# A two-layer hybrid attention trunk on one core: small softmax operations moved to ScalarE

## The chip, the cores and the metric

The kernel runs on 1 core of one Trainium2 chip. The metric is device time in microseconds (us) of one execution; the profile is of one execution, with the time of every instruction on the five engines: TensorE (PE, with its weight loads as PEld), VectorE (DVE), ScalarE (ACT), GpSimd (POOL) and SyncE (SP, which here issues the DMAs).

## What is computed

Two layers of a decoder trunk on 512 tokens of 1024 channels, in float32. Each layer normalizes and modulates its input, projects it once (8608 columns), and feeds two attention branches and their gates:

```python
# branch A: 3 groups of 8 heads x 64, (window, dilation) = (128,1), (512,4), (2048,16)
s = where(valid, q @ k.T * 64**-0.5 + bias, -1e30)
m = max(s); p = exp(s - m); l = sum(p)
o = (p / l) @ v;  lse = m + log(l)
y_a = sum(o * softmax(lse over the 3 groups)) * silu(a_z)
# branch B: 16 heads, 64 + 32 rotary, low-rank q and kv
y_m = softmax(causal((q_nope @ k_nope.T + q_rope @ k_rope.T) * 96**-0.5)) @ v * silu(m_z)
# merge
x = x + gate * ((sigmoid(g_a) * (y_a @ W_a) + sigmoid(g_m) * (y_m @ W_b)) @ W_o)
```

## The kernel before

Every float32 factor of a matmul is kept as two parts, a rounded high part and the difference to it, and a product is three matmuls (line 166). A weight tile of 128 columns is loaded by SP (`stage`, two buffers), its high part `wh` is made on ScalarE or VectorE (lines 203, 205), its low part `wl` mostly on GpSimd by a subtraction of 128x1024 (line 206), and its 24 matmuls of 512 columns go into one of two PSUM banks called `pj`.

The bank is then read out in two parts. For a key of groups 1 and 2 (lines 663 to 667) that is four operations: the high half of head 0 on ScalarE (`kb`, line 211), its low half on VectorE (line 667), then the high half of head 1 (line 213) and its low half (line 667), both on VectorE. Only then can the next but one projection have the bank.

Branch A runs per layer in four pairs of heads, j = 0 to 3 (`a_attn`). `a_scores` makes the scores in `s` banks; VectorE adds the bias, writes `p` and takes the row maxima (lines 782, 800), a small operation scales them by -1/8 into `m0` and `m12` (lines 784, 802), and ScalarE takes the exponential with these as bias (lines 786, 806). `a_factors` joins the three groups. Groups 1 and 2 hold their tokens in another order (by phase p instead of by block qb), so their statistics `ml` (maxima and sums) are reordered by `swap_blocks` into `mn`, and later the factors `fn` into `fp`: 16 copies of 32 partitions each time, 32x4 or 32x2 elements (line 815), dealt to the engines by the string `SW = "GVVV"`: 4 on GpSimd, 12 on VectorE. Between the two swaps stands a chain of small operations of 128x8 elements (lines 834 to 845: `M`, `en`, its exponential on ScalarE at line 838, `L`, `fn`). After the second one `f12` is made and the `p` tiles are scaled (lines 860, 862), transposed (line 869) and multiplied with v.

Branch B runs 16 heads per layer (`m_head`), each in four blocks of rows. Per block VectorE adds the mask and takes the maximum `m` (line 1101), a 128x1 product with the row's scale gives `nms` (line 1102), and ScalarE takes the exponential with it as bias (line 1103).

The order of instructions on each engine is not the order of the code: a list scheduler with a model of the engines sets it when the program is built, and priorities and tile pools steer it. Each engine then works through its own list in order and stops at the first instruction whose inputs are not there.

Of the kernel before, what the change touches and what calls it, by code (L numbers as in the profile page):

```python
# [13 lines left out]
AF = mybir.ActivationFunctionType  # L14
ALU = mybir.AluOpType
# [33 lines left out]
GP = (0, 0, 1, 0, 0)  # L49
KD = "GG"  # L50
LE = "GV"
SW = "GVVV"
YZ = "GGV"
ENG = dict(first="AGAG", qk="AAAG", v="AGAV", az="GGVA", lat="VVGG", mz="VGVA", gate="VAVA", uq="AGGG", ukv="VVAG",
           q="AGAG", y="VGAV", out="AAVV", mr="GGAA", wo="VGVV", K="AAVV", kr="GGGV", sq="AGGG", kv="VA", pk="AV",
# [5 lines left out]
SA = 0.125  # L61
# [76 lines left out]
def trunk(ctx, tc, x, positions, w_ada, w_in, w_uq, w_ukv, w_out_a, w_out_b, w_o, rel_bias, vecs, cst, ohb, bmask, out):  # L138
    nc = tc.nc
    V, A, G, T = nc.vector, nc.scalar, nc.gpsimd, nc.tensor  # L140
# [15 lines left out]
    def t2(tag, dt=F32, shape=(128, 512)):  # L156
        return sb.tile(list(shape), dt, tag=tag, name=nm(tag), bufs=BUFS[tag])

    def small(shape, tag, bufs=2, dt=F32):
        return sb.tile(list(shape), dt, tag=tag, name=nm(tag), bufs=bufs)  # L160

    def bank(tag, dt=F32):
        return ps.tile([128, 512], dt, tag=tag, name=nm(tag), bufs=PB[tag])

    def mm(o, l, r, start, stop):
        T.matmul(o, l, r, start=start, stop=stop, skip_group_check=True)  # L166
# [292 lines left out]
    for t in range(NT):  # L459
        for i in range(2):  # L460
# [12 lines left out]
            for k in range(2):  # L473
                e = V.tensor_copy if k % 2 else A.copy
# [127 lines left out]
    def layer(l, xT, hT):  # L602
# [156 lines left out]
        def a_scores(j, qk, stat):  # L759

            bts = [t2("bias") for _ in range(2)]
            for e in range(2):
                dma(bts[e], btile[2 * j + e])
            m0, l0, m12, l12 = stat
            pps = [[], []]

            def scores(o, q, k):
                mm(o, q[0], k[0], True, False)
                mm(o, q[0], k[1], False, False)
                mm(o, q[1], k[0], False, True)  # L770

            for e in range(2):
                x0 = small([128, 4], "x0")
                sp = [bank("s"), bank("s")]
                pp = [t2("p"), t2("p")]
                for qb, pc, c0, n in G0_BLOCKS:
                    o = sp[pc][:, c0:c0 + n]
                    k0 = 128 * (qb - 1) if n == 256 else 0
                    qt = qk[0][0][e][:, 128 * qb:128 * qb + 128]
                    mm(o, qt, qk[0][1][e][:, k0:k0 + n], True, False)  # L780
                    mm(o, qt, qk[0][1][2][e][:, k0:k0 + n], False, True)
                    V.tensor_tensor_reduce(pp[pc][:, c0:c0 + n], o, bts[e][:, 256 - n:256], 1.0, -3e38,
                                           ALU.add, ALU.max, x0[:, qb:qb + 1])
                V.tensor_scalar(m0[:, e, :], x0, -SA, None, ALU.mult)
                for qb, pc, c0, n in G0_BLOCKS:
                    A.activation(pp[pc][:, c0:c0 + n], pp[pc][:, c0:c0 + n], AF.Exp, bias=m0[:, e, qb:qb + 1],
                                 scale=SA, accum_out=l0[:, e, qb:qb + 1])
                pps[e] += pp
            for g in (1, 2):
                x12 = small([128, 2, 4], "x12")  # L790
                pt = [t2("p"), t2("p")]
                for p2 in range(2):
                    o = bank("s")
                    for p in (2 * p2, 2 * p2 + 1):
                        sl = slice(128 * p, 128 * p + 128)
                        scores(o[:, 256 * (p % 2):256 * (p % 2) + 256], [a[:, sl] for a in qk[g][0]],
                               [a[:, p].rearrange("d e i -> d (e i)") for a in qk[g][1]])
                        for e in range(2):
                            c0 = 256 * (p % 2) + 128 * e
                            V.tensor_tensor_reduce(pt[e][:, sl], o[:, c0:c0 + 128], bts[e][:, 128 + 128 * g:256 + 128 * g],  # L800
                                                   1.0, -3e38, ALU.add, ALU.max, x12[:, e, p:p + 1])
                V.tensor_scalar(m12[:, g - 1], x12, -SA, None, ALU.mult)
                for e in range(2):
                    for p in range(4):
                        sl = slice(128 * p, 128 * p + 128)
                        A.activation(pt[e][:, sl], pt[e][:, sl], AF.Exp, bias=m12[:, g - 1, e, p:p + 1],  # L806
                                     scale=SA, accum_out=l12[:, g - 1, e, p:p + 1])
                    pps[e].append(pt[e])
            return pps

        def swap_blocks(dst, src):
            for qb in range(4):
                for p in range(4):
                    c = SW[(4 * qb + p) % len(SW)]
                    (A.copy if c == "A" else (G if c == "G" else V).tensor_copy)(  # L815
# [39 lines left out]
        def scaled(p, blocks, engines):  # L855

            for (c0, n, f), e in zip(blocks, engines):
                sl = p[:, c0:c0 + n]
                if e == "A":
                    A.activation(sl, sl, AF.Copy, scale=f)  # L860
                else:
                    (V if e == "V" else G).tensor_scalar(sl, sl, f, None, ALU.mult)

        def transposed(srcs):

            n = 128 * len(srcs)
            tp = bank("t")
            for b, s in enumerate(srcs):
                T.transpose(tp[:, 128 * b:128 * b + 128], s, eye)  # L869
            h, lo = t2("pth", F32R), t2("ptl", F32R)  # L870
            hi_copy(h[:, :n], tp[:, :n], "pt")
            V.tensor_tensor(lo[:, :n], tp[:, :n], f32(h[:, :n]), ALU.subtract)  # L872
            return h, lo

        def cols(a, c0):
            return a[:, c0:c0 + 128]

        def pv_block(o, vtile, hh, ph, pl, last):

            c = 128 * hh + 64 * (hh % 2)  # L880
            vh, vl = vtile[:, c:c + 64], vtile[:, c + 64 - 128 * (hh % 2):][:, :64]
            mm(o, vh, ph, False, False)
            mm(o, vh, pl, False, False)
            mm(o, vl, ph, False, last)
# [54 lines left out]
        q_scale = None  # L939
# [145 lines left out]
        def m_head(q, vts, hh):  # L1085
            qh, ql = q
            kh, kl = K[hh]
            m = small([128, 4], "mm")
            ls = small([128, 4], "ml_")
            nms = small([128, 4], "mn_")  # L1090
            sp = [bank("s") for _ in range(3)]
            pp = [t2("p") for _ in range(3)]
            for qb, pc, c0 in M_BLOCKS:
                n = 128 * qb + 128
                o = sp[pc][:, c0:c0 + n]
                qs = slice(128 * qb, 128 * qb + 128)
                mm(o, qh[:, qs], kh[:, :n], True, False)
                mm(o, qh[:, qs], kl[:, :n], False, False)
                mm(o, ql[:, qs], kh[:, :n], False, True)
                pt = pp[pc][:, c0:c0 + n]  # L1100
                V.tensor_tensor_reduce(pt, o, mask[:, 512 - n:512], 1.0, -3e38, ALU.add, ALU.max, m[:, qb:qb + 1])  # L1101
                V.tensor_tensor(nms[:, qb:qb + 1], m[:, qb:qb + 1], q_scale[1][:, qb:qb + 1], ALU.mult)
                A.activation(pt, pt, AF.Exp, bias=nms[:, qb:qb + 1], scale=q_scale[0][:, qb:qb + 1], accum_out=ls[:, qb:qb + 1])
            V.reciprocal(ls, ls)
            for i in range(3):
                scaled(pp[i], [(c0, 128 * qb + 128, ls[:, qb:qb + 1]) for qb, pc, c0 in M_BLOCKS if pc == i], SM[i])
            at = {qb: (pp[pc], c0) for qb, pc, c0 in M_BLOCKS}
            o = bank("o")
            vs = slice(128 * hh, 128 * hh + 128)
            def blocks(kb):  # L1110
                return [cols(at[qb][0], at[qb][1] + 128 * kb) for qb in range(kb, 4)]

            def pv(kb, ph_, pl_, last=False):
                mm(o[:, 128 * kb:], vts[kb][:, vs], ph_, kb == 0, False)
                mm(o[:, 128 * kb:], vts[kb][:, vs], pl_, False, last)

            h, lo = transposed(blocks(0))
            pv(0, h, lo)
            h, lo = transposed(blocks(1) + blocks(3))
            pv(1, h[:, :384], lo[:, :384])  # L1120
            pv_block(o[:64, 384:], vts[3], hh, h[:, 384:], lo[:, 384:], False)
            h, lo = transposed(blocks(2))
            pv(2, h[:, :256], lo[:, :256], True)
            return o
# [90 lines left out]
        for n in range(16):  # L1215
            q, i, e = n // 4, n // 2 % 2, n % 2
# [31 lines left out]
        for c2 in range(4):  # L1248
            parts = []
            for a, wv, yv, tag in ((0, w_out_a, yar, "zs"), (1, w_out_b, ymr, "yy")):  # L1250
                gs = []
                for i in range(2):
                    col = 256 * c2 + 128 * i
                    g = t2(tag)
# [119 lines left out]
```

## Time and profile before

| | us |
|---|---|
| median of 3 runs | 1466.23 |
| lowest, highest | 1463.68, 1473.56 |
| the profiled execution: its own time | 1475.04 |
| the profiled execution: span of its instructions | 1473.3 |

Times below come from the profiled execution, in us from the start of its span. Busy shares of its span: PE 92%, DVE 69%, ACT 42%, POOL 41%. [...] Branch A lies at about 140 to 450 us in layer 0 and 850 to 1150 in layer 1, the heads of branch B at 450 to 625 and 1150 to 1325.

### The profile page before, as it was taken

To read this page: it belongs to the slowest core of one execution; us is meant where nothing else is said; L and a number is where in the kernel's file an instruction comes from. 1 tells how busy PE (TensorE), PEld (TensorE's weight loads), DVE (VectorE), ACT (ScalarE), POOL (GpSimd) and SP (SyncE) were. 2 spreads that over 40 slices of the span, in tenths; PEclk is the share of its full clock that TensorE was granted. 3 is DMA by queue.
4 is the path that set the end of the run, shared out by engine and by line. 5 is a ranking of instruction groups with operands and counts; after the bars stand their busy time and mean duration, and the time that the engine had idled before them with its cause. 6 is when DMAs were issued, how large, how long until landed. Compare 5 with 4: busy or idle time off the path is not lost.

```text
span 1473.3 us, 21395 instructions
## 1 busy us (share of the span) xinstructions
PE 1355.9 (92%) x7327; PEld 1164.8 (79%) x7327; DVE 1011.8 (69%) x2477; ACT 624.0 (42%) x1493; POOL 602.9 (41%) x495
## 2 busy tenths in 40 slices
PE   4998798999998999999988999899999899999997
PEld 4787686897887777888888987689788777787877
DVE  7788769346766788855689347734676688885563
ACT  3424552335345767621034254333534576762101
POOL 5423435334563342345434344523456334234530
PEclk7999999999999999999999999999999999999998
DMA  9676414323244333455644232223324433345541
GB/s 323 224 241 187 142 44 122 90 79 86 58 129 116 96 84 111 128 173 164 202 150 131 81 97 73 79 77 90 88 58 129 118 95 86 99 127 186 166 138 58
DMA packets 236677, 181.48 MB, mean 123 GB/s; under 512 B 16410, under 2 KB 204224, under 8 KB 236568
## 3 DMA queue, kind: packets, MB, share of 16 engines
q1 hardware_dynamic: 236568, 180.11, 40.8%
q8 instruction: 58, 0.95, 0.3%
q14 instruction: 51, 0.42, 0.1%
HBM read 150.60 MB, written 23.17 MB: 118 GB/s over the span
## 4 chain that ended last, share of the span: by engine, by line
PE 59%; DVE 22%; DMA 6%; ACT 5%; issue 4%; POOL 3%; SPq 1%; DVEq 0%; ACTq 0%; POOLq 0%
PE pj L166 41%; PE s L166 12%; PE o L166 4%; PE t L869 3%; ACT p L806 2%; DVE mn L815 2%; DMA stage<-in_w_o 2%; POOL wl L206 2%; DVE p L1101 1%; DVE lat L286 1%; DVE ptl L872 1%; DMA v<-in_w_ada 1%; DVE wh L205 1%; DVE fp L815 1%; DVE kb L1043 1%
## 5 line engine op out<-in xcount | busy, mean ns | idle before, releaser
L206 POOL TENSOR_TENSOR wl<-stage,wh 128x1024 fp32r<-128x1024 f32 (+1 forms) x134 | 316.3, 2361 | 350.7 <-ACT wh L203 184.7
L166 PE MATMUL pj<-hTh,wh 128*128 128x512 f32 (+1 forms) x864 | 346.2, 401 | 49.3 <-DVE kb L667 24.8
L166 PE MATMUL pj<-hTl,wh 128*128 128x512 f32 (+1 forms) x864 | 340.4, 395 | 0.0
L166 PE MATMUL pj<-hTh,wl 128*128 128x512 f32 (+1 forms) x848 | 336.7, 397 | 0.0
L166 PEld LDWEIGHTS pj<-hTh,wh 128*128 128x128 f32 x864 | 166.9, 193 | 87.7 <-issue 36.9
L166 PEld LDWEIGHTS pj<-hTl,wh 128*128 128x128 f32 x864 | 166.9, 193 | 32.7 <-issue 0.3
L166 PEld LDWEIGHTS pj<-hTh,wl 128*128 128x128 f32 x848 | 164.2, 194 | 29.1 <-issue 0.2
L203 ACT ACTIVATE wh<-stage 128x1024 fp32r<-128x1024 f32 (+1 forms) x84 | 85.1, 1014 | 151.2 <-PE s L166 62.5
L872 DVE TENSOR_TENSOR ptl<-t,pth 128x512 fp32r<-128x512 f32 (+2 forms) x160 | 95.9, 615 | 42.1 <-ACT pth L211 41.6
L211 ACT ACTIVATE pth<-t 128x512 fp32r<-128x512 f32 (+2 forms) x160 | 80.8, 537 | 60.1 <-PE t L869 58.9
L166 PE MATMUL s<-kb,qh 128*128 128x256 f32 (+3 forms) x384 | 86.2, 317 | 9.3 <-DVE mm L1101 3.6
L166 PE MATMUL o<-pth,v 128*64 128x128 f32 (+3 forms) x496 | 88.6, 255 | 2.9 <-DVE kh L923 1.9
L166 PE MATMUL o<-ptl,v 128*64 128x128 f32 (+2 forms) x320 | 77.0, 274 | 6.7 <-DVE ptl L872 6.3
L869 PE MATMUL t<-eye_r,p 128*128 128x128 f32 x560 | 79.8, 275 | 2.2 <-DVE ptl L872 1.0
L166 PEld LDWEIGHTS s<-kb,qh 128*128 128x128 f32 x384 | 64.9, 189 | 20.6 <-DVE mm L1101 6.1
L1101 DVE CUSTOM_DVE_ANT_0 p<-s,cs 128x512 f32<-128x512 f32 (+3 forms) x128 | 58.6, 484 | 25.9 <-PE s L166 25.5
L205 DVE CAST wh<-stage 128x1024 fp32r<-128x1024 f32 (+1 forms) x77 | 57.5, 747 | 22.2 <-DMA stage<-in_w_in 11.9
L166 PEld LDWEIGHTS o<-pth,v 128*64 128x64 f32 (+1 forms) x496 | 63.7, 150 | 9.1 <-DVE kh L923 3.2
L869 PEld LDWEIGHTS t<-eye_r,p 128*128 128x128 f32 x560 | 63.3, 140 | 9.0 <-DVE ptl L872 2.4
L166 PE MATMUL pj<-wh,hTh 128*128 128x256 f32 (+1 forms) x192 | 65.1, 340 | 5.7 <-DVE kb L667 3.5
L286 DVE SCALAR_TENSOR_TENSOR lat<-lat,cact,lat 128x512 f32<-128x512 f32 x56 | 60.8, 1085 | 7.7 <-ACT lat L277 4.6
L166 PE MATMUL pj<-wh,hTl 128*128 128x256 f32 (+1 forms) x192 | 63.6, 331 | 0.0
(712 smaller groups left out, 3096.9 us busy)
## 6 DMA issues: line engine op xcount, KB each, us to landing
stage<-in_w_in SPq DMA_DIRECT2D x118, 512.0 KB
lat<-in_w_ada SPq DMA_DIRECT2D x64, 256.0 KB
v<-in_w_ada SPq DMA_DIRECT2D x32, 256.0 KB
stage<-in_w_in SPq DMA_DIRECT2D x32, 256.0 KB
gd<-gt SPq DMA_DIRECT2D x32, 256.0 KB
stage<-in_w_out_b SPq DMA_DIRECT2D x16, 512.0 KB
stage<-in_w_o SPq DMA_DIRECT2D x16, 512.0 KB
p<-yd SPq DMA_DIRECT2D x24, 256.0 KB
```

What stands on the lines that cost most here:

```text
L166: T.matmul(o, l, r, start=start, stop=stop, skip_group_check=True)
L203: A.activation(dst_h, src, AF.Copy)
L205: hi.tensor_copy(dst_h, src)
L206: (lo or G).tensor_tensor(dst_l, src, f32(dst_h), ALU.subtract)
L211: A.activation(dst, src, AF.Copy)
L286: V.scalar_tensor_tensor(acc, st, cact[:, k:k + 1], side if k == ne + np_ else acc, ALU.mult, ALU.add)
L806: A.activation(pt[e][:, sl], pt[e][:, sl], AF.Exp, bias=m12[:, g - 1, e, p:p + 1], scale=SA, accum_out=l12[:, g - 1, e, p:p + 1])
L815: (A.copy if c == "A" else (G if c == "G" else V).tensor_copy)(dst[32 * p:32 * p + 32, :, qb], src[32 * qb:32 * qb + 32, :, p])
L869: T.transpose(tp[:, 128 * b:128 * b + 128], s, eye)
L872: V.tensor_tensor(lo[:, :n], tp[:, :n], f32(h[:, :n]), ALU.subtract)
L1043: V.tensor_tensor(kl_[d, :], pj[d, :], f32(kh_[d, :]), ALU.subtract)
L1101: V.tensor_tensor_reduce(pt, o, mask[:, 512 - n:512], 1.0, -3e38, ALU.add, ALU.max, m[:, qb:qb + 1])
```

## The change

Three kinds of small operation go to ScalarE: all 16 copies of each of the 16 swaps (192 leave VectorE, 64 GpSimd), the 32 scalings of maxima of branch A, and the 128 products of branch B. The values stay the same.

```diff
-SW = "GVVV"
+SW = "A"
@@ a_scores
-                V.tensor_scalar(m0[:, e, :], x0, -SA, None, ALU.mult)
+                A.activation(m0[:, e, :], x0, AF.Copy, scale=-SA)
-                V.tensor_scalar(m12[:, g - 1], x12, -SA, None, ALU.mult)
+                A.activation(m12[:, g - 1], x12, AF.Copy, scale=-SA)
@@ m_head
-                V.tensor_tensor(nms[:, qb:qb + 1], m[:, qb:qb + 1], q_scale[1][:, qb:qb + 1], ALU.mult)
+                A.activation(nms[:, qb:qb + 1], m[:, qb:qb + 1], AF.Copy, scale=q_scale[1][:, qb:qb + 1])
```

The scheduler sets the rest anew. VectorE's list at the first swap of layer 0 (j = 0) before; `kb` is the key of group 1 that leaves the bank `pj_1742`:

```order
L830 TENSOR_TENSOR ml_1356<-tl_1362 128x8
L815 COPY mn_1365<-ml_1356 32x4 x12
L667 TENSOR_TENSOR kb_451<-pj_1742,kb_448 64x4x128
L213 CAST kb_448<-pj_1742 64x4x128
L834 TENSOR_TENSOR M_1382<-m_264_1235,mn_1365 128x8
L667 TENSOR_TENSOR kb_451<-pj_1742,kb_448 64x4x128
```

and now:

```order
L830 TENSOR_TENSOR ml_1356<-tl_1362 128x8
L667 TENSOR_TENSOR kb_451<-pj_1742,kb_448 64x4x128
L213 CAST kb_448<-pj_1742 64x4x128
L667 TENSOR_TENSOR kb_451<-pj_1742,kb_448 64x4x128
L834 TENSOR_TENSOR M_1382<-m_264_1235,mn_1365 128x8
L836 TENSOR_TENSOR en_1384<-M_1382,m_264_1235 128x8
```

The three operations that empty the bank follow `ml` directly, and `M` comes behind them. It is the same at j = 2 of layer 0 and at j = 0 and 2 of layer 1. ScalarE's list at the first of these places, as a difference:

```order
 L211 ACTIVATE kb_448<-pj_1742 64x4x128
 L203 ACTIVATE wh_2244<-stage_2242 128x1024
+L815 COPY mn_1365<-ml_1356 32x4 x16
 L211 ACTIVATE qh_1802<-pj_1777 128x512
 L203 ACTIVATE wh_2281<-stage_2279 128x1024
 L838 ACTIVATE en_1384<-en_1384 128x16
+L815 COPY fp_1395<-fn_1393 32x2 x16
 L860 ACTIVATE p_1323<-p_1323,f_301_1414 128x128 x2
```

The swap stands behind the key's copy `kb`. At j = 1 of layer 0 it stands in front of it, and one more copy (line 300), which waits for TensorE, stands inside the swap. ScalarE's list at the first two heads of branch B now (`mn__826` and `mn__861` are the products of heads 0 and 1, `kb` and `qh` are copies out of `pj` banks; before, the rows of line 1102 were not there):

```order
L1102 ACTIVATE mn__826_4387<-mm_4385,nrq_2750 128x1
L628 ACTIVATE gt_4382<-pj_4351 128x512
L1102 ACTIVATE mn__826_4387<-mm_4385,nrq_2750 128x1 x2
L1103 ACTIVATE p_4391,ml__825_4386<-p_4391,mn__826_4387,rq_2749 128x512
L1103 ACTIVATE p_4392,ml__825_4386<-p_4392,mn__826_4387,rq_2749 128x384
L1103 ACTIVATE p_4393,ml__825_4386<-p_4393,mn__826_4387,rq_2749 128x256
L211 ACTIVATE kb_4243<-pj_4460 64x512
L1102 ACTIVATE mn__861_4561<-mm_4559,nrq_2750 128x1
L1102 ACTIVATE mn__826_4387<-mm_4385,nrq_2750 128x1
L211 ACTIVATE qh_4475<-pj_4468 64x512
```

Three products of a head now stand in front of its first exponential, which waited for one before; two copies out of `pj` banks come behind them.

## Rows read from the trace of the kernel before

**Rows 1.** The page's busy times of the whole span by engine (us, share of the span, instructions).

```profile
PE 1355.9 (92%) x7327; PEld 1164.8 (79%) x7327; DVE 1011.8 (69%) x2477; ACT 624.0 (42%) x1493; POOL 602.9 (41%) x495
```

**Rows 2.** The waits of PE over the whole span, by what ended them: us in total, times, longest.

```profile
PE pj L166 <- DVE kb L667: 28.3, 10, 6.6
```

**Rows 3.** PE in order of time: the first matmuls after seven of these waits (start, duration, engine, line, operation, count; in brackets the idle time before and its releaser). The places are j = 0, 1, 1 and 2 of layer 0, then j = 0, 1 and 2 of layer 1.

```profile
182.43 0.76 PE L166 MATMUL pj<-hTh,wh 128*128 128x512 f32 x1 [6.64 <-DVE kb L667]
...
235.60 0.76 PE L166 MATMUL pj<-hTh,wh 128*128 128x512 f32 x1 [3.86 <-DVE kb L667]
...
251.93 0.47 PE L166 MATMUL pj<-hTh,wh 128*128 128x512 f32 x1 [1.80 <-DVE kb L667]
...
367.52 0.76 PE L166 MATMUL pj<-hTh,wh 128*128 128x512 f32 x1 [2.85 <-DVE kb L667]
...
887.61 0.47 PE L166 MATMUL pj<-hTh,wh 128*128 128x512 f32 x1 [2.38 <-DVE kb L667]
...
952.80 0.47 PE L166 MATMUL pj<-hTh,wh 128*128 128x512 f32 x1 [4.08 <-DVE kb L667]
...
1067.30 0.77 PE L166 MATMUL pj<-hTh,wh 128*128 128x512 f32 x1 [2.85 <-DVE kb L667]
```

**Rows 4.** Stretches just behind these waits: from and to, length, then busy us and instructions of PE, PEld, DVE, ACT and POOL, the granted clock, the share of the DMA engines and GB/s.

```profile
182.43:185.88 3.45, 3.45 (x8) 2.77 (x9) 3.17 (x18) 0.22 (x1) 1.52 (x6) 0.50 0.08 24
235.60:240.49 4.89, 4.89 (x12) 3.83 (x13) 4.86 (x15) 1.17 (x3) 1.65 (x1) 0.50 0.75 210
367.52:373.61 6.09, 6.09 (x14) 4.76 (x15) 5.46 (x29) 1.93 (x6) 3.23 (x8) 0.50 0.01 3
889.02:892.44 3.42, 3.42 (x9) 2.66 (x9) 3.27 (x12) 0.40 (x1) 3.20 (x7) 0.50 0.00 0
...
1067.30:1073.34 6.04, 6.04 (x14) 4.75 (x15) 5.41 (x29) 1.88 (x6) 3.19 (x8) 0.50 0.01 3
```

**Rows 5.** All engines but PE and PEld in order of time at the swap of layer 0, j = 0 (columns as in rows 3).

```profile
173.00 0.59 ACT L211 ACTIVATE kb<-pj 64x512 fp32r<-64x512 f32 x1
...
173.22 0.17 DVE L830 TENSOR_TENSOR ml<-tl 128x8 f32<-128x8 f32 x1
173.42 6.52 DVE L815 COPY mn<-ml 32x4 f32<-32x4 f32 x12
...
174.67 2.37 POOL L206 TENSOR_TENSOR wl<-stage,wh 128x1024 fp32r<-128x1024 f32 x1 [0.38 <-POOL mn L815]
...
177.22 2.34 POOL L206 TENSOR_TENSOR wl<-stage,wh 128x1024 fp32r<-128x1024 f32 x1 [0.18 <-ACT wh L203]
179.97 0.68 DVE L667 TENSOR_TENSOR kb<-pj,kb 64x512 fp32r<-64x512 f32 x1
180.67 0.69 DVE L213 CAST kb<-pj 64x512 fp32r<-64x512 f32 x1
...
181.59 0.69 DVE L667 TENSOR_TENSOR kb<-pj,kb 64x512 fp32r<-64x512 f32 x1
```

**Rows 6.** DVE in order of time at the swaps of j = 1 and then of j = 2 of layer 0: what comes just before the swap, and the last or first read of the key's bank behind it.

```profile
226.55 0.17 DVE L830 TENSOR_TENSOR ml<-tl 128x8 f32<-128x8 f32 x1
...
234.76 0.69 DVE L667 TENSOR_TENSOR kb<-pj,kb 64x512 fp32r<-64x512 f32 x1
...
359.94 0.17 DVE L830 TENSOR_TENSOR ml<-tl 128x8 f32<-128x8 f32 x1
...
365.06 0.68 DVE L667 TENSOR_TENSOR kb<-pj,kb 64x512 fp32r<-64x512 f32 x1
```

**Rows 7.** Line 815 by engine and form: duration in ns, shortest, median and longest, first and last start.

```profile
L815 DVE COPY mn<-ml x96: 160/164/2392, 173.4 to 1112.9; 32x4 f32<-32x4 f32 x96
L815 DVE COPY fp<-fn x96: 157/161/2344, 184.2 to 1120.4; 32x2 f32<-32x2 f32 x96
```

**Rows 8.** Groups by line and form: count, busy us in total, mean ns of one, idle time of the engine before them and its releaser.

```profile
L860 ACT ACTIVATE p<-p,f 128x128 f32<-128x128 f32 x32 | 10.2, 391 | 36.9 <-DVE f L852 36.9
...
L802 DVE TENSOR_SCALAR m<-x 128x8 f32<-128x8 f32 x16 | 7.8, 489 | 0.2
...
L784 DVE TENSOR_SCALAR m<-x 128x4 f32<-128x4 f32 x16 | 5.8, 365 | 0.2
```

**Rows 9.** ScalarE's operation of line 838, without a scale or bias from a tile (columns as in rows 7).

```profile
L838 ACT ACTIVATE en<-en x8: 215/216/217, 182.6 to 1117.0; 128x16 f32<-128x16 f32 x8
```

**Rows 10.** Four operations of line 860, with a scale from a tile, in a row (columns as in rows 3).

```profile
188.44 1.28 ACT L860 ACTIVATE p<-p,f 128x128 f32<-128x128 f32 x4 [5.63 <-DVE f L852]
```

**Rows 11.** The two stretches of branch B's heads (columns as in rows 4).

```profile
450.00:625.00 175.00, 163.74 (x886) 137.13 (x885) 140.64 (x372) 117.50 (x283) 59.35 (x47) 1.00 0.37 105
1150.00:1325.00 175.00, 163.72 (x886) 137.40 (x886) 140.72 (x372) 117.47 (x282) 59.19 (x47) 1.00 0.35 102
```

**Rows 12.** Line 1102 alone in the first of these stretches: DVE's busy us and count, the granted clock, the DMA share and GB/s.

```profile
450.00:625.00 175.00, 21.93 (x64) 1.00 0.37 105
```

**Rows 13.** PE's waits from 450 to 625 us (columns as in rows 2): the largest and the smallest of the nine that end by DVE, 8.9 us together, and the only one that ends by ACT.

```profile
PE o L166 <- DVE ptl L872: 2.9, 5, 1.0
...
PE s L166 <- ACT kb L211: 1.0, 1, 1.0
...
PE pj L166 <- DVE v L618: 0.2, 1, 0.2
```

**Rows 14.** DVE in order of time at j = 1 of layer 1: the operation that takes `mn`, and the one after it.

```profile
940.49 1.91 DVE L834 TENSOR_TENSOR M<-m,mn 128x8 f32<-128x8 f32 x1
942.44 0.17 DVE L836 TENSOR_TENSOR en<-M,m 128x8 f32<-128x8 f32 x1
```

## Prediction

> **What bounds the kernel now.** I read the page's busy times first: TensorE is busy 92% of the span, every other engine at most 69% [rows 1]. So an edit that takes work off VectorE, ScalarE or GpSimd pays only where TensorE stands still for them. The second view is the list of TensorE's waits. Its largest entry by far is 28.3 us in ten waits for line 667, VectorE's read of a key out of a `pj` bank [rows 2]. The third view, TensorE in order of time, gives the places: seven of the ten are 24.5 us together, and they lie at the swaps of j = 0, 1 and 2 of both layers [rows 3]. The fourth view, stretches behind these waits, shows a second price: TensorE resumes at a granted clock of 0.50, the lower level, and stays there for 3.4 to 6.1 us [rows 4]. At half speed half of such a stretch is lost.
>
> The fifth view is all engines at one swap. The key's first part is copied by ScalarE at 173.00 to 173.59, and VectorE could have read the rest of the bank from then on. But in its list the twelve copies of the swap come first. They take 6.52 us, from 173.42 to 179.94, and two subtractions of GpSimd run in that time (174.67 to 177.04, 177.22 to 179.56). Only then do the three reads of 0.68, 0.69 and 0.69 us come, the last one ending at 182.28 [rows 5]; TensorE resumes at 182.43 [rows 3]. Twelve undisturbed copies would take 12 x 0.164 = 2.0 us; the median copy takes 164 ns and the longest 2392 [rows 7], about what one of GpSimd's subtractions takes. A small VectorE operation thus waits out a GpSimd operation that has begun.
>
> [...]
>
> **The change part by part.** *Swaps.* ScalarE's price per copy is not in the trace. The nearest row is line 838, 216 ns for 128x16 without a scale from a tile [rows 9]. Four operations of line 860, 391 ns each [rows 8], take 1.28 us in a row [rows 10], so neighbours overlap by (4 x 0.391 - 1.28) / 3 = 0.09 us. Sixteen copies then cost 16 x 0.12 = 2.0 us from below and 16 x 0.216 = 3.5 us from above. Twelve on VectorE now cost 2.0 undisturbed and 6.5 disturbed, so a swap itself gets neither much shorter nor longer. What counts is who stands behind it. In the new lists of j = 0 and 2 in both layers, ScalarE copies the key before the swap, and VectorE reads the bank directly behind `ml`, before `M`.
>
> At j = 0 of layer 0 VectorE can begin at 173.6 and be done after 2.06 us, at 175.7; TensorE's last matmul before its wait is 182.43 - 6.64 = 175.8. The wait goes. At j = 2, `ml` ends at 360.11 [rows 6], the reads end at 362.2, and TensorE gets there at 367.52 - 2.85 = 364.7: it goes too. I take the same for j = 0 and 2 of layer 1. The four waits are 6.64 + 2.85 + 2.38 + 2.85 = 14.7 us [rows 3]. If TensorE doesn't stop, I take it that the clock doesn't fall, which gives half of 3.45 + 6.09 + 3.42 + 6.04, or 9.5 us [rows 4]. Together **24.2 us off**.
>
> At j = 1 of layer 0 the swap stands before the key's copy in ScalarE's new list. `ml` ends at 226.72 [rows 6]; 3.5 us for the swap, some 0.6 for the key's copy and 2.1 for VectorE's reads bring the bank to about 232.9, against 235.45 now: 2.5 us off, and I take 3 for a little of the slow stretch. From both sides: nothing, if the copy inside the swap that waits for TensorE comes late, and 3.86 + 4.89 / 2 = 6.3. **3 off.** At j = 1 of layer 1, and at 251.93, the bank that is late belongs to the second key, behind the second swap. Its copy on ScalarE now stands behind that swap: I take nothing; the bounds are 4.08 + 1.80 off and as much on.
>
> *What is late next.* The second swap is sixteen copies on one engine (2.0 to 3.5 us) in place of a median twelve (2.0 to 2.3), and at the four places where TensorE will arrive early, the second key is copied behind it. I put back 1.2 us at each, the difference of the upper ends: **5 us on**. From below it is nothing, where projections with ready weights cover it; from above all of the 24.2 comes back.
>
> *Scaled maxima.* 32 operations and 7.8 + 5.8 = 13.6 us leave VectorE [rows 8]; ScalarE needs the same value next, and makes it in 0.2 us. The cover is TensorE's projections. I take 0, between 13.6 off and 32 x 0.2 = 6.4 on.
>
> *Products of branch B.* Per stretch of 175 us VectorE is busy 140.6 and ScalarE 117.5 [rows 11], and line 1102 takes 21.9 of VectorE's time for 64 products [rows 12], or 343 ns apiece. On ScalarE they take 0.216 to 0.391 us each (the upper row has a scale from a tile, as they have, but 128 columns), 14 to 25 us, so ScalarE goes to 75 to 81% and VectorE falls to 68%. TensorE waits for VectorE 8.9 us per stretch [rows 13]. From below that is 17.8 us off for both stretches; from above the 25 us come in series with what TensorE waits for, 50 us on. In the new list three products stand before a head's first exponential, and copies out of `pj` banks wait behind them; against that, each such copy's other half is VectorE's. I take **4 off**, about a quarter of the lower bound, since the waits that are left are waits for VectorE.
>
> **Sum:** -24.2 - 3 + 5 - 4 = -26.2 us on the profiled execution's 1475.0, or 1448.8. That execution lies 8.8 above the median of the runs; I forecast their median: 1466.2 - 26.2 = **1440**.
>
> **Rivals.** *Given back.* TensorE comes earlier to the second key, or to weights that are not split yet, and stops there. For it: the waits at 251.93 and 952.80 are of this kind already. Against it: at 360 to 362 us and later there are slack bank reads, and GpSimd's copies, which stood before its subtractions, are gone. Only the waits at 235.60 and a little of branch B remain as gains: 5 us, 1461.
>
> *Slower: small operations in series on ScalarE.* Place: the heads of branch B. A product must end before its exponential on the same engine begins, and the copies of transposed tiles and keys stand behind both. It decides if these copies, not VectorE's halves, become the last thing that TensorE waits for; then 64 x 0.391 = 25 us come on in each stretch, and with the gains of the swaps (22) the time is 1466 + 50 - 22 = 1494. For it: ScalarE's share rises to as much as 81%. Against it: only 1.0 us of TensorE's waits there ends by ScalarE now [rows 13], and a fifth of its time stays free.
>
> [...]
>
> *All waits for VectorE go.* The 28.3 of line 667, half of the slow stretches shown, 11.9, and the 17.8 of branch B: 58 us, 1408. Against it: the second keys' list order.
>
> **How the numbers follow.** Forecast 0.55, given back 0.20, slower 0.13, all waits gone 0.12. A measurement of this kernel can tell about 1% from no change, 14.7 us. Faster by more than that is nearly all of the forecast (0.52) and the last rival: 0.64. Within 1%: the rest of the forecast, most of the given-back case and a mild form of the slower one, 0.25. Slower: 0.11. The range 1414 to 1475 leaves out half of the last rival and most of the slower one, under 2 in 10.
>
> **What would show it.** Right: in the profile after, TensorE's waits for line 667 shrink from 28.3 to under 12 us, the stretches at clock 0.50 behind j = 0 and 2 are gone, ScalarE's swap takes 2 to 3.5 us with no copy above 0.4 us. Wrong: waits of the same length at the same places that end by ScalarE's `kb` or by `qh`; in branch B, more than 10 us of TensorE's waits per stretch, ending by ScalarE's `pth` or `kb`. The forecast fails if the four waits don't go, or if branch B gets longer than 175 us by more than 10.

## The result and the profile after

The changed kernel takes 1444.32 us (median of 4 runs, 1439.8 to 1448.21) against 1465.62 (4 runs): a ratio of 0.9843, 95% interval 0.9819 to 0.9866, 21 us less. The forecast was 1440, in a range of 1414 to 1475. The profiled execution took 1442.84 us, 32.2 less than that of before; the medians differ by 21.3, so some 11 us between the two profiles are taken as no effect of the change. Most of that is found between the layers, where the profile of before loses 7.2 us to that of after: its clock is 0.50 for 3.41 us from 762.73 and for 6.83 us from 807.10. The profiles of `e1_swaps` and `e9_gate_early` below have the longer stretch too, the others neither; each of these three executions is slower than every other one of its kernel, so the stretch seems to come and go with the execution, which one profile for each kernel can't show.

The page's busy times of the changed kernel (columns as in [rows 1]) and TensorE's largest waits that the argument needs (as in [rows 2]):

```profile
PE 1343.7 (93%) x7327; PEld 1157.1 (80%) x7327; DVE 929.8 (65%) x2125; ACT 704.8 (49%) x1909; POOL 588.2 (41%) x431
```

```profile
PE pj L166 <- DVE kb L667: 10.1, 7, 2.4
PE pj L166 <- DVE v L715: 9.3, 5, 5.8
PE pj L166 <- ACT gt L628: 9.2, 2, 4.6
```

82 us have left VectorE and 81 have come to ScalarE. What the time follows is the first wait: 28.3 us then [rows 2], 10.1 now. The third is new: `gt` is the tanh of a gate (line 628) that ScalarE makes from a `pj` bank, and in the kernel before these waits were 3.3 us in four.

The first swap of layer 0, j = 0, in order of time; it answers to [rows 5]:

```profile
171.04 0.59 ACT L211 ACTIVATE kb<-pj 64x512 fp32r<-64x512 f32 x1
171.26 0.17 DVE L830 TENSOR_TENSOR ml<-tl 128x8 f32<-128x8 f32 x1
171.67 0.68 DVE L667 TENSOR_TENSOR kb<-pj,kb 64x512 fp32r<-64x512 f32 x1 [0.24 <-ACT kb L211]
172.36 0.69 DVE L213 CAST kb<-pj 64x512 fp32r<-64x512 f32 x1
172.48 3.29 ACT L815 COPY mn<-ml 32x4 f32<-32x4 f32 x16
172.66 2.40 POOL L206 TENSOR_TENSOR wl<-stage,wh 128x1024 fp32r<-128x1024 f32 x1 [4.61 <-ACT wh L203]
173.09 0.69 DVE L667 TENSOR_TENSOR kb<-pj,kb 64x512 fp32r<-64x512 f32 x1
175.81 0.17 DVE L834 TENSOR_TENSOR M<-m,mn 128x8 f32<-128x8 f32 x1 [2.02 <-ACT mn L815]
```

VectorE begins to read the bank 0.24 us after `ml` and is done at 173.78; before, `ml` ended at 173.39 and the bank was free at 182.28. ScalarE's sixteen copies take 3.29 us although a GpSimd subtraction runs from 172.66 to 175.06. TensorE doesn't stop here; the ten microseconds from 173.78 run at a clock of 1.00, as at j = 2 of layer 1 (columns as in [rows 4]). Matmuls of 512 columns start 0.23 us apart here (174.48 to 177.43), where in the profile of before, at 0.50, they started 0.43 us apart (183.00 to 185.56), so close to half of such a stretch is lost:

```profile
173.78:183.78 10.00, 10.00 (x48) 8.29 (x47) 6.10 (x17) 6.54 (x28) 5.15 (x4) 1.00 0.38 105
...
1035.00:1045.00 10.00, 10.00 (x49) 8.32 (x49) 7.85 (x26) 6.07 (x27) 5.58 (x6) 1.00 0.24 63
```

Line 815 by form (columns as in [rows 7]); no copy is long any more:

```profile
L815 ACT COPY mn<-ml x128: 182/196/199, 172.5 to 1085.1; 32x4 f32<-32x4 f32 x128
L815 ACT COPY fp<-fn x128: 190/192/197, 180.7 to 1090.8; 32x2 f32<-32x2 f32 x128
```

What is late next is the second key at j = 0 of layer 0 (188.42; those of j = 2 are late by 0.9 and 1.0 us), the first key of j = 1 in both layers (2.4 and 2.0 us), and, largest, the gate at j = 3 (397.92; its twin in layer 1 lasts 4.6 us too). TensorE in order of time, j = 0 and 3 of layer 0 and j = 1 of layer 1 (as in [rows 3]):

```profile
188.42 0.60 PE L166 MATMUL pj<-hTh,wh 128*128 128x512 f32 x1 [2.10 <-DVE kb L667]
...
397.92 0.80 PE L166 MATMUL pj<-hTh,wh 128*128 128x512 f32 x1 [4.62 <-ACT gt L628]
...
911.22 0.47 PE L166 MATMUL pj<-hTh,wh 128*128 128x512 f32 x1 [1.96 <-DVE kb L667]
```

The clock of 0.50, which stood behind j = 0 and 2 before, now stands behind the second key of j = 0 for 3.41 us and at the two places of j = 3 for 6.83 us each:

```profile
188.60:192.01 3.41, 3.41 (x9) 2.63 (x9) 1.55 (x6) 0.27 (x1) 3.41 (x2) 0.50 0.15 29
...
396.81:403.64 6.83, 5.72 (x14) 4.52 (x15) 3.29 (x6) 4.19 (x19) 2.36 (x1) 0.50 0.26 79
1079.48:1086.31 6.83, 6.05 (x14) 4.79 (x15) 3.50 (x6) 3.87 (x19) 2.28 (x1) 0.50 0.27 79
```

Why the gate is late is read from ScalarE's list (some rows of the profile at 397 us):

```profile
393.37 0.21 ACT L802 ACTIVATE m<-x 128x8 f32<-128x8 f32 x1 [1.03 <-DVE x L800]
393.61 0.40 ACT L806 ACTIVATE p<-p,m 128x128 f32<-128x128 f32 x1
...
396.32 0.39 ACT L806 ACTIVATE p<-p,m 128x128 f32<-128x128 f32 x1
396.71 0.58 ACT L617 ACTIVATE zs<-pj 128x512 f32<-128x512 f32 x1
397.18 0.20 ACT L827 ACTIVATE ed<-ed 128x16 f32<-128x16 f32 x1
397.29 0.58 ACT L628 ACTIVATE gt<-pj 128x512 f32<-128x512 f32 x1
```

TensorE's last matmul before its wait is at 393.3, and the bank is full then; but the gate's tanh stands behind eight exponentials, and these behind a scaled maximum that ScalarE now makes itself after waiting for VectorE. In the kernel before, the corresponding tanh stood between the first eight exponentials of j = 3 and the last eight, which start at 407.45:

```profile
405.10 0.57 ACT L628 ACTIVATE gt<-pj 128x512 f32<-128x512 f32 x1
```

The start of TensorE's n-th matmul, after minus before, gives the account by place (the orders of the two differ a little, so a single line is good to about a microsecond):

```
n      before us   after - before   place
500      140.5        +0.1          ahead of j = 0, layer 0
1250     296.9       -12.4          behind j = 0 and 1
1750     395.9       -17.0          behind j = 2
2000     439.7       -12.0          behind j = 3: 5.0 given back
3500     737.9       -14.2          behind branch B
4250     870.3       -21.4          between the layers (the clock above)
5000    1010.1       -29.9          behind j = 0 and 1, layer 1
5500    1110.3       -35.5          behind j = 2
5750    1156.9       -28.6          behind j = 3: 6.9 given back
7250    1453.5       -32.3          end
```

Branch B, per stretch of 175 us, and line 1102 on ScalarE (busy time and count, clock, DMA) answer to [rows 11, 12]:

```profile
450.00:625.00 175.00, 165.64 (x907) 139.71 (x906) 124.31 (x305) 131.00 (x346) 60.94 (x47) 1.00 0.40 114
1150.00:1325.00 175.00, 167.02 (x901) 140.47 (x900) 124.39 (x289) 118.87 (x306) 62.60 (x47) 1.00 0.41 119
```

```profile
450.00:625.00 175.00, 16.02 (x61) 1.00 0.40 114
```

A product costs ScalarE 16.02 / 61 = 263 ns of busy time there, against 343 on VectorE. That is less than a product lasts, 277 to 301 ns, since neighbours in a row overlap by some 95 ns.

### The profile page after: what moved, and what is told of

It reads as the page before. It is cut to its first block, busy times and chain, and to the rows that moved or that the text cites. A ratio compares the mean times of both kernels' runs of the same rounds, so it can differ in the third digit from the quotient of the medians.

```text
span 1441.0 us, 21364 instructions
## 1 busy us (share of the span) xinstructions
PE 1343.7 (93%) x7327; PEld 1157.1 (80%) x7327; DVE 929.8 (65%) x2125; ACT 704.8 (49%) x1909; POOL 588.2 (41%) x431
## 4 chain that ended last, share of the span: by engine, by line
PE 71%; DVE 13%; DMA 5%; issue 4%; ACT 3%; POOL 2%; SPq 1%; DVEq 0%; POOLq 0%; ACTq 0%
PE pj L166 50%; PE s L166 12%; PE o L166 5%; PE t L869 4%; DMA stage<-in_w_o 2%; DMA stage<-in_w_in 1%; DVE lat L286 1%; POOL wl L206 1%; DVE zs L286 1%; DMA ql<-pl 1%; DVE kb L667 1%; DVE p L392 1%; DMA lat<-in_w_ada 1%; DVE p L1101 1%; DVE yy L923 1%
## 5 line engine op out<-in xcount | busy, mean ns | idle before, releaser
L166 PE MATMUL pj<-wl,hTh 128*128 128x256 f32 (+1 forms) x192 | 62.7, 328 | 0.1
```

## The experiments

**Each part alone.** The swaps (`e1_swaps`) are `SW = "A"` and nothing else:

```diff
-SW = "GVVV"
+SW = "A"
```

> The swaps alone on ScalarE (line 815), the scalings of maxima and the products of branch B as before. Theory: the gain of the change is that TensorE no longer waits for keys that VectorE reads behind a swap; then this alone gives most of the 21 us, ratio 0.984 to 0.990, and the waits for line 667 fall from 28.3 to under 14 us. Rival (VectorE's load in branch B was the gain): under 5 us, ratio 0.997 or more.

1442.27 us, ratio 0.9833 (0.9811 to 0.9855): the swaps alone are the whole gain. TensorE's waits for line 667:

```profile
PE pj L166 <- DVE kb L667: 11.4, 5, 4.0
```

Between matmuls 1750 and 2000, at j = 3, this kernel loses 0.4 us where the whole change loses 5.0.

The scalings (`e2_scalings`) are lines 784 and 802 of the change alone.

> The 32 scalings of maxima alone on ScalarE (lines 784, 802). Theory: hidden under projections, within 4 us of before, ratio 0.997 to 1.003. Rival (ScalarE's exponentials wait 38 us for these small operations, and this is what TensorE lacks): 8 us or more off, ratio 0.995 or less.

1469.22 us, 1.0011 (0.9994 to 1.0028): nothing, but as a sum of two things. By matmul 1750 it is 5.9 us ahead of before, by 2000 only 1.0. Its waits show both; the two of the second entry, 4.0 us each, stand at j = 3 of the two layers:

```profile
PE pj L166 <- DVE kb L667: 19.7, 10, 4.7
...
PE pj L166 <- ACT gt L628: 7.9, 2, 4.0
```

The products (`e3_products`) are line 1102 of the change alone.

> The 128 products of branch B alone on ScalarE (line 1102). Theory: the waits for VectorE there are short, so 2 to 4 us off, ratio 0.997 to 0.999. Rival A (VectorE's load): 8 us or more off, about 0.994. Rival B (series on ScalarE): slower, 1.003 or more.

1460.5 us, 0.9963 (0.995 to 0.9976), or 5.4 us, a little more than the theory's 2 to 4; the waits for line 667 stay at 27.1. The first stretch of branch B:

```profile
450.00:625.00 175.00, 165.27 (x897) 139.40 (x898) 124.11 (x311) 130.73 (x348) 59.41 (x47) 1.00 0.37 107
```

ScalarE is at 75% of it, the lower end of the forecast's 75 to 81, and the kernel is faster, so the slower rival falls. The three ratios multiply to 0.981, the change has 0.984; with intervals of 0.002 about each, that alone doesn't show whether the parts add up (`e5_no_scalings` below does).

**The shut-out alone.** `e4_reduce` leaves every engine's list as it was before, and replaces only the form of VectorE's twelve copies of a swap: a reduction by maximum over an axis of one element, which gives the same values.

```diff
-                    (A.copy if c == "A" else (G if c == "G" else V).tensor_copy)(
-                        dst[32 * p:32 * p + 32, :, qb], src[32 * qb:32 * qb + 32, :, p])
+                    (G.tensor_copy if c == "G" else lambda d, s: V.tensor_reduce(d, s, mybir.AxisListType.X, ALU.max))(
+                        dst[32 * p:32 * p + 32, :, qb], src[32 * qb:32 * qb + 32, :, p:p + 1] if c == "V" else src[32 * qb:32 * qb + 32, :, p])
```

> The kernel before, in the same order on every engine, but the 12 copies of a swap that VectorE makes are reductions (maximum over an axis of one element, the same values) in place of copies. Theory (a swap is long because a VectorE copy is shut out while a GpSimd operation runs, and a reduction is not): none of line 815 on VectorE is longer than 0.4 us, a swap takes some 2.2 us in place of 3.7, waits for line 667 fall from 28.3 to 12 to 20, time down by 6 to 14 us, ratio 0.990 to 0.996. Rival (only the place in VectorE's list counts, or every small operation is shut out): long ones of up to 2.4 us stay, no change within 3 us, ratio 0.998 to 1.002.

1450.83 us, 0.9891 (0.9869 to 0.9912), a little more than the theory's 0.990 to 0.996, and the waits for line 667 are 12.9. In the trace every engine's list is that of before, instruction by instruction. The reductions by form, and VectorE at the first swap:

```profile
L815 DVE TENSOR_REDUCE mn<-ml x96: 149/153/160, 171.6 to 1084.5; 32x4 f32<-32x4 f32 x96
L815 DVE TENSOR_REDUCE fp<-fn x96: 146/149/155, 179.5 to 1091.6; 32x2 f32<-32x2 f32 x96
```

```profile
171.43 0.17 DVE L830 TENSOR_TENSOR ml<-tl 128x8 f32<-128x8 f32 x1
171.63 1.99 DVE L815 TENSOR_REDUCE mn<-ml 32x4 f32<-32x4 f32 x12
173.65 0.68 DVE L667 TENSOR_TENSOR kb<-pj,kb 64x512 fp32r<-64x512 f32 x1
```

Same place, same order, 1.99 us in place of 6.52 [rows 5]: the long copies waited for GpSimd, and that alone is 1.1 of the 1.7% that the swaps gave in `e1_swaps`. The rest would then be the order, the bank's reads ahead of the swap; that was not tried by itself. No reduction is above 160 ns, though 27 of the 192 run beside a GpSimd subtraction; of the 192 copies of before 64 ran beside one, and took 160 to 2392 [rows 7].

**Off VectorE, but not to ScalarE.** `e7_swaps_on_gpsimd` has `SW = "G"` and nothing else.

> The kernel before with all 16 copies of each swap on GpSimd, scalings and products unchanged. Theory (the loss is VectorE's copies waiting for GpSimd's subtractions in front of the bank's reads): the reads of the key at the first swap follow ml directly, so TensorE's waits for line 667 fall from 28 to under 20 us; but the copies now stand behind a subtraction in GpSimd's own list and delay the next one, so mn comes 2 to 5 us later than by ScalarE and later weights are late: 1448 to 1460, between the swaps on ScalarE (1442) and before. Rival (ScalarE itself is what helps, for instance because its copies are faster): no gain, 1463 to 1475, and waits for line 667 of 25 us or more.

1455.18 us, 0.9938 (0.9922 to 0.9954), the time that the theory gave. The waits for line 667 are the shortest of all, 7.9 us, and waits that end by GpSimd are new (`p`) or longer (`wl`, 2.7 before):

```profile
PE t L869 <- POOL p L862: 9.2, 5, 3.0
...
PE pj L166 <- DVE kb L667: 7.9, 6, 4.4
...
PE pj L166 <- POOL wl L206: 4.1, 3, 1.9
```

So it is not ScalarE's speed (its copy, 196 ns, is slower than GpSimd's 184) but the clear way to the bank's reads. More than half of the 1.67% is given back, since GpSimd comes late to the factors' multiplications and to the weights. The theory had one detail wrong: `mn` is complete 3.6 to 5.3 us behind `ml`, against 3.3 to 4.4 in `e1_swaps`, so hardly later. What is late comes behind it: in six of the eight swaps VectorE's `en` of line 836 takes 2.3 us in place of 0.17; in all six a GpSimd subtraction has begun 0.15 us before it and ends 0.02 us before it does. The second swap then takes 3.8 to 7.1 us in place of 3.3.

**Undoing the scalings.** `e5_no_scalings` is the change with lines 784 and 802 as before.

> The changed kernel with one part undone: swaps and products stay on ScalarE, the 32 scalings of maxima go back to VectorE. Theory (the scalings put a wait in front of the gate's tanh at j = 3 and so give back about 5 us per layer): TensorE's wait of 4.6 us for gt (line 628) behind 396 us and its twin in layer 1 are gone, and the time is 1434 to 1440, or 0.979 to 0.983 of before, below the changed kernel's 0.9843. Rival (the scalings do no harm beside the swaps; what was lost at j = 3 comes from the swaps themselves): the waits for gt stay at 4 us or more and the ratio is 0.984 to 0.987.

1444.09 us, 0.9851 (0.9831 to 0.987): the same as the change, so the theory's time was missed, although its mechanism is in the profile. The waits for `gt` are down to 0.3 us, and this kernel is 5.3 us ahead of the change behind j = 3. It loses 9.4 us against it between matmuls 3000 and 3250, behind branch B of layer 0, where other weight parts are late. Its waits of TensorE from 625 to 660 us (the changed kernel has one there, 0.5 us):

```profile
PE s L166 <- DVE wl L206: 3.2, 2, 2.9
PE pj L166 <- DVE v L206: 1.9, 2, 1.7
```

with 3.41 us at a clock of 0.50 behind them. One place was mended and another, far away, came up in the new lists. What is left of the lead in this profile, the fastest of its five runs, is 4.3 us; the medians have none. So the parts don't add up: swaps and products together gain 1.49%, where their two ratios multiply to a gain of 2.03%.

**The gate alone.** `e9_gate_early` keeps the whole change and only lets the two gate projections behind `a_attn(3)` have an earlier priority:

```diff
-        gates(GS[0])
+        tc.cur_priority += -200; gates(GS[0]); tc.cur_priority -= -200
```

> The changed kernel whole, with the two gate projections behind a_attn(3) given an earlier priority, so that in ScalarE's list the tanh of the gate gt_4101 and of zs_4033 stands in front of the last eight exponentials of j = 3, not behind them. Theory (what is given back at j = 3 is the gate's place in ScalarE's list behind exponentials that wait for VectorE, not the scalings as work): TensorE's two waits for gt of 4.6 us are gone although the scalings stay on ScalarE, and the profile gains 8 to 13 us on the changed one; the median 1432 to 1441, ratio 0.977 to 0.983. Rival (the scalings are late by themselves, and the exponentials would come late wherever the gate stands): a wait of the same length ends by the exponentials' readers or by gt at another place, ratio 0.984 or more.

1431.07 us (5 runs, 1428.73 to 1437.79), 0.975 (0.9734 to 0.9765): the fastest of all, and more than the theory's 0.977 to 0.983. ScalarE's rows at j = 3 show `gt` and `zs` ahead of the exponentials:

```profile
391.38 0.60 ACT L628 ACTIVATE gt<-pj 128x512 f32<-128x512 f32 x1 [0.95 <-PE pj L166]
...
393.45 0.60 ACT L617 ACTIVATE zs<-pj 128x512 f32<-128x512 f32 x1 [0.53 <-POOL yy L934]
394.55 0.21 ACT L802 ACTIVATE m<-x 128x8 f32<-128x8 f32 x1 [0.50 <-DVE x L800]
394.79 0.40 ACT L806 ACTIVATE p<-p,m 128x128 f32<-128x128 f32 x1
```

Two waits for the next gate, 4.1 us together, are left of 9.2; its tanh (404.7) stands behind the sixteen copies of the swap (401.3 to 404.6) in ScalarE's list. The ratios stand 0.93% apart, or 13.7 us. By the matmuls this kernel still gives back 1.3 and 2.8 us at j = 3, where the change gives back 5.0 and 6.9, so 7.8 us are found there; this profile, the slowest of its five runs, is 5.0 us ahead of the change in all and loses 4.1 of its lead between the layers (the longer stretch at 0.50). Where the rest of the 13.7 comes from isn't shown. The scalings are still on ScalarE, so at j = 3 it is the gate's place in the list that cost, not the scalings as work.

**Reductions and products together.** `e6_reduce_products` is `e4_reduce` with line 1102 on ScalarE.

> The kernel before with VectorE's 12 copies of each swap as a reduction by maximum over an axis of one element (no ScalarE in the swaps), and the products of branch B on ScalarE. Theory (what the swaps lose is the time that VectorE's copies are shut out by GpSimd, and that is another place and another cause than branch B): the two add up, 0.9891 x 0.9963 = 0.985, or 1443 to 1448. Rival (the gains share a cause, such as VectorE's total load): not below 0.989, 1450 or more.

1442.44 us, 0.984 (0.9826 to 0.9854), close to the product of the two ratios (0.9854). Every engine's list is that of `e3_products` here, so the reductions alone make the difference between these two: without any swap on ScalarE the kernel is as fast as the change.

`e8_reduce_all` is the same with all sixteen as reductions on VectorE (`SW = "V"`).

> The kernel before with all 16 copies of each swap on VectorE as reductions over an axis of one element (none on GpSimd or ScalarE), and the products of branch B on ScalarE. Theory (the cost of a swap in front of a bank's read is its undisturbed length, GpSimd's four copies are no part of it): four reductions more are 4 x 0.15 = 0.6 us per swap, and no shut-out, so 1438 to 1447, 0.981 to 0.987, the same as with twelve. Rival (GpSimd's four copies are what delays its subtractions and so the weights): faster than with twelve by over 0.5%, 1435 or less.

1460.15 us, 0.9969 (0.9955 to 0.9982): both expectations missed, by 13 us and more. Its reductions are as short as before (median 152 ns), but the lists came out anew, and with them the wait for the gate; between matmuls 1750 and 2000 and between 5500 and 5750 it loses 6.2 and 6.9 us to `e6_reduce_products`.

```profile
PE pj L166 <- DVE kb L667: 17.0, 9, 4.5
PE pj L166 <- ACT gt L628: 10.4, 2, 5.2
```

`e10_reduce_all_gate_early` adds the earlier priority of the gates to that.

> The kernel of 16 reductions on VectorE and the products on ScalarE, with the same earlier priority for the gates. Theory (it lost 18 us to the kernel with 12 reductions because its list put gt_4101 behind the exponentials): the waits for gt of 10.4 us are gone and the time comes back to 1440 to 1449, ratio 0.983 to 0.989. Rival (the four additional reductions themselves are what costs): 1455 or more, ratio 0.993 or more.

1473.41 us, 1.0033 (1.002 to 1.0046). The waits for `gt` are gone, as the theory had it, but the time is the rival's, though not for its reason: four reductions more are 2.65 us a swap in place of 1.99. Part of the loss shows at j = 0 of layer 0, VectorE and then TensorE:

```profile
169.96 2.65 DVE L815 TENSOR_REDUCE mn<-ml 32x4 f32<-32x4 f32 x16
172.63 0.68 DVE L667 TENSOR_TENSOR kb<-pj,kb 64x512 fp32r<-64x512 f32 x1
173.33 0.69 DVE L213 CAST kb<-pj 64x512 fp32r<-64x512 f32 x1
174.06 2.06 DVE L834 TENSOR_TENSOR M<-m,mn 128x8 f32<-128x8 f32 x1
176.15 0.69 DVE L667 TENSOR_TENSOR kb<-pj,kb 64x512 fp32r<-64x512 f32 x1
```

```profile
176.99 0.77 PE L166 MATMUL pj<-hTh,wh 128*128 128x512 f32 x1 [4.66 <-DVE kb L667]
```

`M` stands in front of the bank's last read and takes 2.06 us (a GpSimd subtraction runs from 173.76 to 176.10); in `e6_reduce_products` it stands at the same point of the list and takes 0.22. At j = 3 the loss to `e6_reduce_products` stays at 6.4 and 5.8 us (matmuls 1750 to 2250 and 5500 to 5750), but TensorE now waits for the multiplication of `p` by its factors, 2.1 us at j = 3 of either layer, and in layer 0 3.41 us at a clock of 0.50 stand behind that:

```profile
PE t L869 <- DVE p L862: 5.6, 3, 2.1
```

Another 9.4 us go behind branch B of layer 1, with waits for line 206 as in `e5_no_scalings`. So at j = 3 one late operation went and another came; whether it had been hidden behind the gate or is new with these lists isn't shown. Why `e10_reduce_all_gate_early` is 0.64% (some 9 us) slower than `e8_reduce_all`, and not about equal, stays open beyond these places.

## Why the prediction was right

- *The four waits (-24.2) and what is given back behind the second swap (+5).* The waits at j = 0 and 2 are gone in both layers. Behind them the second keys wait 2.1, 0.9 and 1.0 us, with one stretch of 3.41 us at 0.50, half of it lost: 5.7 us. Matched matmul by matmul around these places, the gains are 4.6, 4.6, 5.3 and 5.7 (matmuls 640 to 750, 1500 to 1750, 4250 to 4500, 5250 to 5500), or some 20 net; the forecast had 19.2. The copies on ScalarE start 206 ns apart and don't overlap, so a swap takes 3.3 us, near the upper of the forecast's 2.0 and 3.5. The clock's part, 9.5 of the 24.2, was needed for that sum: the waits alone are 14.7.
- *j = 1 (-3 and 0).* Too small. The waits of 9.7 us fell to 4.3, and 3.4 us less run at a clock of 0.50: about 7 us by these, 10 by the matmuls (750 to 1250 and 4500 to 5000). In layer 1 the bank's reads follow `ml` directly, where the forecast had looked at the second key alone.
- *Scalings (0).* Right in the sum (`e2_scalings`), wrong in the way: the list that they bring on ScalarE holds the gate's tanh behind exponentials. That is the term I had not written: +12 us (5.0 and 6.9). The step that failed is "the cover is TensorE's projections": a projection also needs its bank emptied, and the engine that empties it was given a wait.
- *Products (-4).* 5.4 us alone; a product cost 263 ns of ScalarE's busy time, inside 216 to 391. Beside the swaps the gain isn't seen in the time (`e5_no_scalings`).
- *Sum.* -20, -7 to -10, +12 and -5 make -20 to -23, beside -21 by the medians. The mechanism of the swaps was right, but that the forecast came out within 4.3 us is partly luck: the missed gain at j = 1 and the missed loss at j = 3 have opposite signs.
- *Rivals.* "Given back" was true in kind and wrong in place: not the second key but the gate, and 12 us, not 22. The slower one fell with `e3_products`. A swap of 3.3 us in place of twelve undisturbed copies (2.0) is 16 x 1.3 = 21 us more work, and `e1_swaps` shows that it doesn't lengthen the time. "All waits go" (1408) was not reached; `e9_gate_early`, at 1431, with one cause of loss removed, went a third of the way from the change towards it.
- *What would show it.* Waits for line 667 under 12 us (10.1), a swap of 3.3 us and no copy above 0.2: these came. The stretches at 0.50 behind the first keys of j = 0 and 2 are gone; one of 3.41 us stands behind the second key of j = 0.

## What to carry to other kernels

A small VectorE operation can cost as much as the GpSimd operation that runs beside it (2.4 us in place of 0.16 here), so look at the longest duration of a group, not only at its median, and at what stands behind it in the list: the operations that empty TensorE's banks should not. Changing the operation's form can help without moving anything, as `e4_reduce` shows (0.9891). And where a scheduler sets the lists, most edits deal them anew: compare the new lists at each read of a bank, since here the place of a gate was worth 7.8 us by the matmuls at j = 3, and the edit that mended it 13.7 by the ratios, of a forecast gain of 26.

## What the runs showed of the hardware

ScalarE's copies took 182 to 199 ns, and the 46 of the 256 that ran beside a GpSimd subtraction 182 to 198; VectorE's of `mn` took 160 to 2392 [rows 7]. The forecast's 2.0 to 3.5 us for a swap took ScalarE's copies as undisturbed, which no row of before shows; here they were. A VectorE operation is still long beside a GpSimd subtraction after the change: not `M` (at most 170 ns in the eight swaps; one took 1.91 us before [rows 14]) but `L` of line 840, 2.36 us at 177.62, during a subtraction that runs from 177.57 to 179.97, against 161 to 169 ns in six of the eight swaps. I had not expected that a reduction of 32x4 elements, 153 ns, would be as cheap as an undisturbed copy (164).
